# Down projection of a ConvFFN: pass order, place of the last split, and banks of the last token tile

## The chip, the core and the metric

The kernel runs on one core of a Trainium2 chip. The metric is the device time of one execution in microseconds; of several runs the median counts. TensorE (PE) multiplies, VectorE (DVE) and ScalarE (ACT) evict, split and normalise, GpSimd (POOL) does little but issue some transfers, and SyncE (SP) issues most of them.

## The reference

One layer of a decoder trunk on 1024 tokens of width 1024 in float32: a mixer (stick-breaking attention and a short convolution, gated and projected), then a ConvFFN. Only the ConvFFN's end is touched by the change:

```python
h = rms_norm(x, norm_ffn_pre[l])
u = causal_dwconv(h @ w_up[l], conv_ffn_w[l])
a, g = jnp.split(u, 2, axis=-1)
f = (jax.nn.gelu(g, approximate=True) * a) @ w_down[l]
x = x + rms_norm(f, norm_ffn_post[l])
```

w_up is 1024 x 5632, w_down 2816 x 1024. So f has 2816 rows of 1024 tokens before the last product, which are 22 k-tiles of 128.

## The kernel before

**Numbers in two halves.** Each float32 operand is scaled by a power of two and split into two float16 tiles: ScalarE copies the high half (line 100), VectorE subtracts it and keeps the low half (line 101). A product of two such operands has three passes over the halves: (0, 0), (0, 1) and (1, 0), which is `PASSES`; the first number is the half of f, the second that of w_down. The scale comes from a sum of squares per partition that a matmul with ones adds over the partitions (line 83, tile `pr`), and two or three small VectorE instructions (lines 90 to 93).

**The up projection.** For each of the 22 k-tiles of f a pair of up products is computed by seven block products of 12 matmuls each (line 1198, tiles `pu<f>a`, `b` and `c`, one PSUM bank each). Their sums are evicted on ScalarE and VectorE (lines 1213 to 1227), convolved (lines 1272 to 1275), passed through GELU (line 1282), multiplied (line 1283), and their squares summed (line 57, `jk_f`). The f tiles stay in float32 until their group is split.

**The down projection in six bursts.** The 22 k-tiles of f are taken in groups of 2, 4, 4, 4, 4 and 4. One call of `down(g)` multiplies a group's k-tiles by their rows of w_down for all eight token tiles, 128 tokens by 1024 columns each, in two banks of 512 columns: 192 matmuls for a group of four, 96 for the group of two. They are the six bursts of this document, the first to the sixth. Group g's f tiles are split by `f_split(g)` and its rows of w_down are loaded and split by `dn_split(g)`; both are called some products ahead of `down(g)`, during the next group's second pair. In the first four bursts ScalarE copies the sums out (line 1097) and transfers add them up in memory (`yd`); in the fifth VectorE adds the sum loaded from there (line 1099), and in the sixth VectorE adds to that, ScalarE squares (line 1101), VectorE multiplies by the gain (line 1103), sums the squares (line 1109), and after the root (lines 229 and 230) adds the residual (line 1113), half a row at a time, and the result goes out (line 1114).

The last three calls of the FFN are, in this order, `down(ng - 2)`, `f_split(ng - 1)` and `down(ng - 1)`: the fifth burst, the split of the last four f tiles, the sixth burst. Before them stand both remaining `dn_split`.

**Buffers.** The rows of w_down are staged in float32 in a pool of four buffers, `ws`, which the weights of the up products use too (line 1059 for w_down, line 114 for w_up). A staging buffer is free again after VectorE has made the low half out of it. All PSUM banks of the FFN, eight of 512 columns, come from one pool, `pz` (line 1005), for the up products as for the bursts and the `pr` sums. Slots of a slab of sixteen hold f tiles, both kinds of split tiles, the sums of the up products, and at the end the gain, the residual and the output tiles.

**What sets the order.** The FFN is written without an order per engine. A planner lists the instructions: an instruction's priority is its place in the program, and each engine takes, in a simulated time, the first one in priority whose operands and buffers are ready. On the chip each engine then runs its list strictly in order. Matmuls that accumulate into one bank keep the order of the program. `high_priority` (line 1201) lifts the evictions of the up products.

## Time and profile before

| | |
|---|---|
| median of 3 runs | 1318.55 us (1317.56 to 1321.24) |
| profiled execution | 1321.92 us |
| its span | 1320.1 us |
| TensorE busy | 1278.1 us, 97% of the span |
| VectorE busy | 995.3 us, 75% |
| ScalarE busy | 807.3 us, 61% |
| burst matmuls | 1056, idle before them 9.9 us |

The profile shows one execution. A group line has the source line, the engine, the operation, output<-inputs by the names of the tiles without their numbers, the shape and the count, then busy time and mean duration in ns, then the engine's idle time just before them and what ended it. A timeline line has the start and the duration in us, then the same, with the idle time before in square brackets. Matmuls overlap one another in the pipeline: the duration of one is longer than the time from one start to the next. A row with several instructions (x186) spans from the first start to the last end.

### The profile page before, as it was taken

The numbers are of one execution on the slowest core, as the hardware profiler recorded it, in microseconds if no ns is written. First come the engines' busy times: TensorE is split into PE (matmuls) and PEld (weight loads), VectorE is DVE, ScalarE is ACT, GpSimd is POOL, SyncE is SP. The second block draws the span as 40 slices with busy tenths as digits, with TensorE's granted clock in tenths as the row PEclk, the third lists the DMA queues.
The fourth block names the chain that finished last, engine by engine and source line by source line (L and its number), as shares of the span: only waits on it lengthen the run. The fifth ranks groups of instructions, "written<-read, shape, count | busy, mean of one in ns | idle before, by whom it ended". The sixth has DMA issues, their size and how long they took to land. (4 is left out here: it accounts for less than half of the span.)

```text
span 1320.1 us, 16773 instructions
## 1 busy us (share of the span) xinstructions
PE 1278.1 (97%) x6465; PEld 583.7 (44%) x6465; DVE 995.3 (75%) x1584; ACT 807.3 (61%) x1146; POOL 48.6 (4%) x69
## 2 busy tenths in 40 slices
PE   5999999999999999999989999999999999999997
PEld 3444444444444444444544444444444444444443
DVE  5568878797877878796888959917955890798758
ACT  6366575657767666755665677646754764676422
POOL 1000000000000000001100000020010002000001
PEclk9999999999999999999999999999999999999999
DMA  7034535454441212513312252373256239512125
GB/s 272 1 70 104 125 78 115 106 111 94 88 120 49 64 62 68 191 49 112 133 59 65 64 223 64 96 128 128 64 130 157 65 96 209 174 64 96 64 75 196
DMA packets 109391, 139.56 MB, mean 106 GB/s; under 512 B 79088, under 2 KB 79088, under 8 KB 109312
## 3 DMA queue, kind: packets, MB, share of 16 engines
q1 hardware_dynamic: 105360, 124.28, 31.3%
q0 software_dynamic: 3952, 14.23, 6.1%
q8 instruction: 50, 0.82, 0.3%
q14 instruction: 29, 0.24, 0.1%
HBM read 94.45 MB, written 25.17 MB: 91 GB/s over the span
## 5 line engine op out<-in xcount | busy, mean ns | idle before, releaser
L1198 PEld LDWEIGHTS <-wh_u 128*128 128x128 f16 x1848 | 178.7, 98 | 217.7 <-issue 4.0
L1093 PE MATMUL pd<-wdh,f 128*128 128x512 f16 x1056 | 233.9, 383 | 9.9 <-DVE wdh L101 5.7
L1093 PEld LDWEIGHTS <-f 128*128 128x128 f16 x1056 | 104.1, 99 | 138.2 <-issue 13.9
L1198 PEld LDWEIGHTS <-wh_g 128*128 128x128 f16 x588 | 56.9, 98 | 68.7 <-issue 0.4
L908 PE MATMUL py<-wh_wo,m 128*128 128x512 f16 x384 | 83.9, 379 | 0.0
L1097 ACT ACTIVATE y<-pd,sd 128x512 f32<-128x512 f32 x64 | 42.3, 693 | 64.7 <-PE pd L1093 58.3
L101 DVE SCALAR_TENSOR_TENSOR wh_u<-ws_u,sc,wh_u 128x1024 f16<-128x1024 f32 (+1 forms) x66 | 72.3, 1102 | 8.9 <-ACT wh_u L100 8.9
L100 ACT ACTIVATE wh_u<-ws_u,sc 128x1024 f16<-128x1024 f32 (+1 forms) x66 | 64.2, 998 | 22.6 <-DVE ws_u L1033 12.6
L535 ACT ACTIVATE R<-z,cz 128x1024 f32<-128x1024 f32 (+3 forms) x48 | 43.2, 899 | 42.4 <-PE z L531 42.3
L549 DVE TENSOR_TENSOR_SCAN R<-R,edge 128x256 f32<-128x256 f32 (+3 forms) x64 | 49.2, 811 | 19.6 <-ACT R L535 19.5
L90 DVE TENSOR_SCALAR sc<-pr 128x1 int32<-128x1 int32 x47 | 6.8, 153 | 75.0 <-PE pr L83 75.0
L1275 DVE SCALAR_TENSOR_TENSOR ugu<-cgu,cw_g,ugu 128x1023 f32<-128x1023 f32 (+1 forms) x44 | 56.4, 1281 | 8.8 <-ACT ugu L1273 8.6
L1275 DVE SCALAR_TENSOR_TENSOR ua<-cau,cw_a,ua 128x1023 f32<-128x1023 f32 (+1 forms) x44 | 56.3, 1279 | 2.0 <-ACT ua L1273 1.8
L908 PEld LDWEIGHTS <-m 128*128 128x128 f16 x384 | 37.5, 98 | 44.1
L549 DVE TENSOR_TENSOR_SCAN R<-R,cy,zero 128x512 f32<-128x512 f32 x32 | 39.3, 1270 | 12.4 <-ACT R L535 12.4
L57 ACT ACTIVATE jk_u<-ws_u 128x1024 bf16<-128x1024 f32 x44 | 46.5, 1056 | 2.7 <-DMA ws_u<-w_up_nt 2.0
L364 PE MATMUL pv<-wh_v,hT 128*128 128x512 f16 x192 | 45.8, 391 | 2.3 <-ACT wh_v L100 1.7
L262 PE MATMUL pq<-hT,wh_q 128*128 128x512 f16 x192 | 44.2, 379 | 2.1 <-ACT hT L251 1.2
L536 ACT ACTIVATE be<-z,cz 128x1024 f32<-128x1024 f32 (+3 forms) x48 | 43.0, 896 | 4.9 <-DVE R L568 4.8
L1273 ACT ACTIVATE ua<-cau,cw_a 128x1024 f32<-128x1024 f32 x22 | 25.1, 1141 | 34.2 <-DVE cau L1225 31.4
L568 DVE TENSOR_TENSOR R<-be,R 128x1024 f16<-128x1024 f32 (+3 forms) x48 | 45.6, 950 | 0.5 <-ACT R L566 0.2
L558 DVE TENSOR_TENSOR be<-be,R 128x1024 f32<-128x1024 f32 (+3 forms) x48 | 45.7, 953 | 0.1
(666 smaller groups left out, 2521.0 us busy)
## 6 DMA issues: line engine op xcount, KB each, us to landing
ws_u<-w_up_nt SPq DMA_DIRECT2D x44, 512.0 KB, 3.5
yd<-y POOLq DMA_DIRECT2D x24, 512.0 KB, 5.7
ds<-w_down SPq DMA_DIRECT2D x22, 512.0 KB, 6.4
wd<-w_down SPq DMA_DIRECT2D x22, 512.0 KB, 3.5
ws_g<-w_in_nt SPq DMA_DIRECT2D x14, 512.0 KB, 3.5
x<-x SPq DMA_DIRECT2D x8, 512.0 KB, 8.7
ws_wo<-w_out SPq DMA_DIRECT2D x8, 512.0 KB, 6.5
xr<-x SPq DMA_DIRECT2D x8, 512.0 KB, 4.2
```

What stands on the lines that cost most here:

```text
L57: self.nc.scalar.activation(self.junk(f"jk_{name}"), src, AF.Square, accum_out=acc)
L100: self.nc.scalar.activation(dst[:, 0, :], src, AF.Copy, scale=s)
L101: self.nc.vector.scalar_tensor_tensor(dst[:, 1, :], src, s, dst[:, 0, :], ALU.mult, ALU.subtract)
L262: nc.tensor.matmul(ps, w[:, wi, ds(k * P, P)], hT[:, hi, k, ds(c * NH, NH)], start=n == 0, stop=n == last)
L364: nc.tensor.matmul(pv, hT[:, hi, k, ds(tt * P, P)], wv[k // 2][:, wi, ds((k % 2) * NH, NH)], start=n == 0, stop=n == 3 * KD - 1)
L549: nc.vector.tensor_tensor_scan(rev, rev, first, 0.0 if u["top"] else carry[tl][:, h, :], ALU.mult, ALU.add)
L558: nc.vector.tensor_tensor(t["be"][:, :, :W], t["be"][:, :, :W], t["R"][:, :, 1:W + 1], ALU.mult)
L568: nc.vector.tensor_tensor(wv[1], be[:, :, :W], wv[0], ALU.subtract)
L908: nc.tensor.matmul(ps, m16[k][:, hi, ds(tt * P, P)], wo[k][:, wi, sl], start=k == 0 and p == 0, stop=k == 7 and p == 2)
L1093: nc.tensor.matmul(ps, f16[g][k][:, hi, ds(tt * P, P)], w[k][:, wi, sl], start=n == 0, stop=n == 3 * GROUPS[g] - 1)
L1198: nc.tensor.matmul(ps, w[wt][:, wi, ds(wc * NH + k * P, P)], self.block(i, hi, k), start=first and n == 0, stop=n == 3 * KH - 1, skip_grou ...
L1275: nc.vector.scalar_tensor_tensor(u[:, lag:], c[:, :T - lag], sm[:, 2 - lag:3 - lag], u[:, lag:], ALU.mult, ALU.add)
```

## The change

Three edits, all in the down projection:

1. In every burst the order of a bank's matmuls changes from "for each k-tile the passes (0, 0), (0, 1), (1, 0)" to "for each pass of (0, 0), (1, 0), (0, 1) all k-tiles", so that the four products with the low half of w_down are the last. In the first token tile the two banks take turns matmul by matmul; in the other tiles one bank follows the other, as before.
2. `f_split` of the last group is called inside the fifth burst, ahead of the third token tile's matmuls, where before it stood behind the burst.
3. In the sixth burst the last token tile has three banks, of 512, 256 and 256 columns, where it had two of 512; each has its own eviction, square, and gain product, and one more small addition joins the third sum of squares.

```diff
-        def down(g):
+        def down(g, within=None):
...
-                for nh in range(2):
-                    ps = self.bank(f"pd{g}_{tt}_{nh}")
-                    sl = ds(nh * NH, NH)
-                    n = 0
-                    for k in range(GROUPS[g]):
-                        for hi, wi in PASSES:
-                            nc.tensor.matmul(ps, f16[g][k][:, hi, ds(tt * P, P)], w[k][:, wi, sl],
-                                             start=n == 0, stop=n == 3 * GROUPS[g] - 1)
-                            n += 1
+                if tt == 2 and within is not None:
+                    within()
+                cols = [(0, NH), (NH, NH // 2), (NH + NH // 2, NH // 2)] if last and tt == 7 else [(0, NH), (NH, NH)]
+                banks = []
+
+                def products(qs, part):
+
+                    for hi, wi in qs:
+                        for k in range(GROUPS[g]):
+                            for n, (c0, cw) in part:
+                                nc.tensor.matmul(banks[n][:, :cw], f16[g][k][:, hi, ds(tt * P, P)],
+                                                 w[k][:, wi, ds(c0, cw)], start=(hi, wi) == (0, 0) and k == 0,
+                                                 stop=(hi, wi) == (0, 1) and k == GROUPS[g] - 1)
+
+                for n in range(len(cols)):
+                    banks.append(self.bank(f"pd{g}_{tt}_{n}"))
+                order = ((0, 0), (1, 0), (0, 1))
+                if tt == 0:
+                    products(order, list(enumerate(cols)))
+                for n, (c0, cw) in enumerate(cols):
+                    ps, sl = banks[n][:, :cw], ds(c0, cw)
+                    if tt > 0:
+                        products(order, [(n, (c0, cw))])
...
                 if last:
                     nc.vector.tensor_tensor(sm_[:, 0:1], sm_[:, 3:4], sm_[:, 4:5], ALU.add)
+                    if len(cols) > 2:
+                        nc.vector.tensor_tensor(sm_[:, 0:1], sm_[:, 0:1], sm_[:, 5:6], ALU.add)
...
-        down(ng - 2)
-        f_split(ng - 1)
+        down(ng - 2, lambda: f_split(ng - 1))
         down(ng - 1)
```

## The prediction

> **What bounds the kernel now.** I read the page first, then the groups by shape, then TensorE in order of time around the six bursts of the down projection, then its clock there.

> ```profile
> span 1320.1 us, 16773 instructions
> PE 1278.1 (97%) x6465; PEld 583.7 (44%) x6465; DVE 995.3 (75%) x1584; ACT 807.3 (61%) x1146; POOL 48.6 (4%) x69
> L1093 PE MATMUL pd<-wdh,f 128*128 128x512 f16 x1056 | 233.9, 383 | 9.9 <-DVE wdh L101 5.7 <-ACT f L100 2.3 <-DVE cau L1225 1.5
> ```

> TensorE is busy 97% of the span, so a microsecond in which it stands still is a microsecond of the kernel. The bursts' matmuls lose 9.9 us to waits, 5.7 of it for the low half of w_down. The timeline of TensorE shows where (start, duration, count, idle before):

> ```profile
> 745.03 1.24 PE L1093 MATMUL pd<-wdh,f 128*128 128x512 f16 x5
> 747.74 0.38 PE L1093 MATMUL pd<-wdh,f 128*128 128x512 f16 x1 [1.47 <-DVE cau L1225]
> 748.94 5.73 PE L1093 MATMUL pd<-wdh,f 128*128 128x512 f16 x18 [0.82 <-DVE wdh L101]
> 754.50 0.81 PE L1198 MATMUL pu4a<-hA,wh_u 128*128 128x512 f16 x3
> ...
> 842.72 1.46 PE L1093 MATMUL pd<-wdh,f 128*128 128x512 f16 x6
> 844.98 40.30 PE L1093 MATMUL pd<-wdh,f 128*128 128x512 f16 x186 [0.81 <-DVE wdh L101]
> ...
> 957.79 1.46 PE L1093 MATMUL pd<-wdh,f 128*128 128x512 f16 x6
> 961.13 17.00 PE L1093 MATMUL pd<-wdh,f 128*128 128x512 f16 x78 [1.88 <-DVE wdh L101]
> ...
> 1073.94 1.46 PE L1093 MATMUL pd<-wdh,f 128*128 128x512 f16 x6
> 1077.40 41.99 PE L1093 MATMUL pd<-wdh,f 128*128 128x512 f16 x186 [2.00 <-DVE wdh L101]
> ...
> 1226.23 1.89 PE L1093 MATMUL pd<-wdh,f 128*128 128x512 f16 x8 [0.45 <-ACT wdh L100]
> 1228.30 39.87 PE L1093 MATMUL pd<-wdh,f 128*128 128x512 f16 x184 [0.19 <-DVE wdh L101]
> 1268.01 0.17 PE L83 MATMUL pr<-rb,ones 128*128 128x1 bf16 x1
> 1270.45 41.61 PE L1093 MATMUL pd<-wdh,f 128*128 128x512 f16 x192 [2.28 <-ACT f L100]
> ```

> One matmul takes (1268.01 - 1228.30) / 184 = 0.2158 us from start to start. Against that pace the bursts lose, at their heads: first 2.61 (746.11 to 747.74, 747.96 to 748.94), second 0.96 (844.02 to 844.98), third 2.04, fourth 2.16, fifth 0.34 (1227.96 to 1228.30), sixth 2.41. Inside a burst nothing is lost. The clock adds to it; this table of stretches gives after the DVE and ACT columns the granted clock (0.65, 0.54, 1.00), then the DMA share:

> ```profile
> 748.94:752.50 3.56, 3.56 (x11) 1.39 (x11) 3.56 (x5) 2.22 (x3) 0.00 (x0) 0.65 0.64 167
> 1077.40:1080.95 3.55, 3.55 (x10) 1.25 (x10) 3.49 (x4) 1.34 (x2) 0.00 (x0) 0.54 0.57 177
> 1270.45:1312.00 41.55, 41.55 (x192) 18.69 (x192) 34.88 (x62) 13.21 (x32) 4.62 (x7) 1.00 0.50 173
> ```

> After the gaps of the first and fourth burst the clock was down for some 3.55 us, which cost 3.56 x 0.35 = 1.25 and 3.55 x 0.46 = 1.63 us. After the sixth burst's longer gap it was not.

> **Pass order, bursts two to four: a new wait.** A bank's matmuls run in program order. Before, a bank took all three passes of k-tile 0, then of k-tile 1; now it takes f-high x w-high of all four k-tiles before anything else. So the old order needs the low half early, and the new order needs the high halves of k-tiles 2 and 3 early. When do these come? Second burst, all engines:

> ```profile
> 840.73 2.17 ACT L100 ACTIVATE wdh<-wd,sc 128x1024 f16<-128x1024 f32 x2
> 843.64 1.28 DVE L101 SCALAR_TENSOR_TENSOR wdh<-wd,sc,wdh 128x1024 f16<-128x1024 f32 x1
> 844.84 0.69 DVE L1227 TENSOR_TENSOR cgu<-pu7b,cgu 128x512 f32<-128x512 f32 x1
> 844.95 2.12 SPq L1060 DMA_DIRECT2D wd<-w_down  x2
> 848.52 1.15 ACT L100 ACTIVATE wdh<-wd,sc 128x1024 f16<-128x1024 f32 x1 [1.75 <-DMA wd<-w_down]
> 851.14 1.15 ACT L100 ACTIVATE wdh<-wd,sc 128x1024 f16<-128x1024 f32 x1 [1.47 <-DMA wd<-w_down]
> 853.23 0.57 ACT L1213 ACTIVATE cgu<-pu8a 128x512 f32<-128x512 f32 x1
> 857.05 1.27 ACT L1097 ACTIVATE y<-pd,sd 128x512 f32<-128x512 f32 x2 [2.30 <-PE pd L1093]
> ```

> Only two w_down tiles are staged at the start (the four staging buffers also hold the next pair's weights). The load of k-tile 2 leaves at 844.95, just after VectorE's low split of k-tile 0 (843.64 + 1.28 = 844.92) frees its buffer; its high half is there at 848.52 + 1.15 = 849.67, that of k-tile 3 at 852.29. So the low half of k-tile 0, which the edit calls late, comes before the high half of k-tile 2, which it now needs first.

> How much can TensorE do meanwhile? Of the eight banks one holds pu8a through the burst and one pu7b until 844.84 + 0.69 = 845.53: six banks at the start (hence six matmuls before the old wait), then seven. The planner does spread over them: the first finished bank is copied at 857.05, (857.05 - 844.98) / 0.2158 + 6 = 62 matmuls in, where one bank needs 12. Under the old order seven banks hold 7 x 6 = 42 matmuls on k-tiles 0 and 1 (9.1 us); under the new one 7 x 2 = 14 (3.02 us), then nothing until 849.67. Lost: 849.67 - 842.72 - 3.02 = 3.93 us. Seven more matmuls on k-tile 2 (1.51 us) end before k-tile 3's high half: 852.29 - 849.67 - 1.51 = 1.11 more. From there all passes are covered. The same for the third and the fourth burst:

> ```profile
> 962.18 0.69 DVE L1227 TENSOR_TENSOR cgu<-pu11b,cgu 128x512 f32<-128x512 f32 x1
> 964.63 1.15 ACT L100 ACTIVATE wdh<-wd,sc 128x1024 f16<-128x1024 f32 x1 [0.52 <-DMA wd<-w_down]
> 966.77 1.15 ACT L100 ACTIVATE wdh<-wd,sc 128x1024 f16<-128x1024 f32 x1 [0.98 <-DMA wd<-w_down]
> ...
> 1077.26 0.68 DVE L1227 TENSOR_TENSOR cgu<-pu15b,cgu 128x512 f32<-128x512 f32 x1
> 1080.75 1.15 ACT L100 ACTIVATE wdh<-wd,sc 128x1024 f16<-128x1024 f32 x1 [1.63 <-DMA wd<-w_down]
> 1083.02 1.15 ACT L100 ACTIVATE wdh<-wd,sc 128x1024 f16<-128x1024 f32 x1 [1.12 <-DMA wd<-w_down]
> ```

> Third: 965.78 - 957.79 - 3.02 = 4.97 to k-tile 2, then 967.92 - 965.78 - 1.51 = 0.63. Fourth: 1081.90 - 1073.94 - 3.02 = 4.94, then 0.76. At full clock the three lose 13.84 + 2.50 = 16.34 us, where they lost 0.96 + 2.04 + 2.16 + 1.63 = 6.79: 9.55 us worse. With the clock down after each stall the seven k-tile-2 matmuls run at half pace (3.02 us, past k-tile 3's arrival, so the 2.50 vanish) and 1.63 is lost three times: 13.84 + 4.89 = 18.73, 11.94 worse. I take the second: TensorE now does only 3 us of work in the first 7 to 8 us of each burst, emptier than the gaps that brought the clock down before. The first is kept as the bound.

> [...]

> **Bursts one and five.** The first has two k-tiles, the fifth has all four staged:

> ```profile
> 747.45 1.15 ACT L100 ACTIVATE wdh<-wd,sc 128x1024 f16<-128x1024 f32 x1 [1.81 <-DMA wd<-w_down]
> 1225.04 4.25 ACT L100 ACTIVATE wdh<-wd,sc 128x1024 f16<-128x1024 f32 x4
> ```

> In the first the second high half is there at 748.60 instead of the low at 748.94: 0.34 gained, the clock as before. In the fifth the high halves follow each other by 1.06 us while seven banks take 1.51 us of matmuls for each, so the 0.34 us wait goes.

> **The f split inside the fifth burst.** Its sum is ready early:

> ```profile
> 1245.55 0.15 DVE L74 CAST rb<-sc 128x1 bf16<-128x1 f32 x1
> L83 PE MATMUL pr<-rb,ones 128*128 128x1 bf16 x47 | 7.3, 166 | 5.2 <-DVE rb L74 3.8 <-DVE sc_wc L201 1.3
> ```

> The sum's matmul, now ahead of token tile 2 in priority, can go at about 1246 instead of 1268.01; four splits on ACT and DVE then end by about 1255, beside matmuls, and 2.41 us at the sixth burst go. The sum's matmul could itself hold TensorE until the cast: between 0 and 3.6 us (the cast ends at 1245.7; six finished banks, 72 matmuls, could be over at 1242.1). Only two of 47 such matmuls waited in this trace, so I take 0. The f tiles' four slots come free earlier, so the post-norm gain and residual loads behind them only come sooner.

> **Last tile in three banks.** It adds one eviction, square, product and add on 256 or one columns and halves others; 24 matmuls of 256 columns take 12 x 0.2158 us as before, their weight loads hidden as now (18.69 us of loads inside 41.55). The end hangs on VectorE:

> ```profile
> 1312.53 0.74 DVE L1099 SCALAR_TENSOR_TENSOR y<-pd,sd,y 128x512 f32<-128x512 f32 x1
> L373 DVE SCALAR_TENSOR_TENSOR v<-pv,v 128x256 f16<-128x256 f32 x16 | 6.0, 417 | 4.6 <-ACT v L369 4.6
> ```

> The last eviction falls from 0.74 to about 0.42, the square by about 0.2; but another 0.4 eviction and 0.4 product queue ahead of it, and an add of 0.15 behind. Bounds -0.6 to +0.6; I take 0.

> **Sum.** +11.94 - 0.34 - 0.34 - 2.41 = +8.85 us. The profiled execution took 1321.92, 1.82 outside its span and 3.37 over the median; the terms are differences within one execution, so I add them to the median: 1318.55 + 8.85 = 1327.4. At full clock: 1325.0.

> **Rivals.** (a) The planner fills the hole: pu4a's matmuls inside the first burst show that it puts other products there. The decision point is 9.55 - 3.09 = 6.46 us, 2.15 a burst, ten matmuls. With both 12-matmul products (5.18 us) each new hole of at most 5.7 us is all but gone: -6.79 - 3.09 + 0.94 (what is left of 5.60 and 5.70), so 1309.6, faster. With one product: 16.34 - 7.77 - 6.79 - 3.09 = -1.3, 1317.2. Against it: pu8a's next product needs ACT's copy at 853.23, behind both late high halves in ACT's order. (b) The low waits go and no other comes: 1318.55 - 6.79 - 2.61 - 1.25 - 0.34 - 2.41 = 1305.2. For it only that k-tiles 0 and 1 are split before 842.90. (c) The planner's order isn't changed where it matters; bursts one to four wait as before: 1318.55 - 2.75 = 1315.8. (d) It doesn't spread over banks and stands at token tile 0, 4 matmuls in and then two per k-tile: 8.3, 8.8 and 8.9 us at full clock, 26.0 for 16.34: 1334.7 or more; the 62 matmuls speak against it. (e) The sum's matmul holds the fifth burst: 1327.4 + 3.6 = 1331.0.

> **Numbers.** Forecast 0.58; (a) 0.08 with two products, 0.07 with one; (b) 0.06; (c) 0.08; (d) 0.07; (e) 0.06. The forecast's own range is 1323 to 1331; 1311 to 1334 leaves out (b), (d) and a part of (a). About 0.3% (4 us) is what a measurement here tells from no change. Slower by more: 0.58 + 0.07 + 0.06 = 0.71; within: (c) and one product, 0.15; faster: 0.14.

> **What would show it.** In the changed profile, bursts two to four should show TensorE's idle time released by "ACT wdh L100" and no more by "DVE wdh L101", about 14 matmuls before a stall of 2 to 4 us, and a granted clock near 0.5 after it; the sixth burst should follow the fifth without a gap, the sum's matmul standing inside the fifth. I am wrong if the second burst's 192 matmuls take no more than 42.4 us from its first matmul, or if products of the next pair stand in the holes.

## The result, and the profile after

The changed kernel takes 1341.51 us (median of 4 runs, 1339.47 to 1343.38) where the kernel before takes 1318.62: a ratio of 1.0171, 95% interval 1.0155 to 1.0188. It is 22.9 us slower; forecast were 8.9 us slower, with a range from 1311 to 1334. The direction was right and the size was not.

The page of the changed kernel and the group of its burst matmuls of 512 columns (L1097 there is L1093 of before):

```profile
span 1341.6 us, 16801 instructions
PE 1286.1 (96%) x6477; PEld 586.6 (44%) x6477; DVE 996.5 (74%) x1587; ACT 807.5 (60%) x1148; POOL 47.9 (4%) x69
L1097 PE MATMUL pd<-wdh,f 128*128 128x512 f16 x1044 | 238.1, 390 | 15.6 <-ACT wdh L100 9.2 <-DVE cgu L1242 4.9 <-DVE cau L1240 1.5
```

The low half of w_down (DVE wdh) is gone from the waits, as the change wants it. In its place stand 9.2 us for the high half (ACT wdh) and 4.9 us for a bank. The bursts in order of time:

```profile
749.20 5.34 PE L1097 MATMUL pd<-wdh,f 128*128 128x512 f16 x24 [0.56 <-ACT wdh L100]
...
841.30 3.45 PE L1097 MATMUL pd<-wdh,f 128*128 128x512 f16 x14
848.29 41.45 PE L1097 MATMUL pd<-wdh,f 128*128 128x512 f16 x178 [3.54 <-ACT wdh L100]
...
962.25 2.75 PE L1097 MATMUL pd<-wdh,f 128*128 128x512 f16 x12
967.28 0.59 PE L1097 MATMUL pd<-wdh,f 128*128 128x512 f16 x2 [2.27 <-DVE cgu L1242]
970.23 40.23 PE L1097 MATMUL pd<-wdh,f 128*128 128x512 f16 x178 [2.36 <-ACT wdh L100]
...
1082.97 2.75 PE L1097 MATMUL pd<-wdh,f 128*128 128x512 f16 x12
1088.31 0.59 PE L1097 MATMUL pd<-wdh,f 128*128 128x512 f16 x2 [2.59 <-DVE cgu L1242]
1091.15 41.20 PE L1097 MATMUL pd<-wdh,f 128*128 128x512 f16 x178 [2.25 <-ACT wdh L100]
...
1239.19 11.05 PE L1097 MATMUL pd<-wdh,f 128*128 128x512 f16 x48 [0.45 <-ACT wdh L100]
1258.55 0.16 PE L83 MATMUL pr<-rb,ones 128*128 128x1 bf16 x1 [8.31 <-DVE rb L74]
1258.57 75.25 PE L1097 MATMUL pd<-wdh,f 128*128 128x512 f16 x348
```

Two things are to be seen. Bursts two to four do 14 matmuls and then stand still until k-tile 2's high half is there (the third and the fourth also wait after 12 of the 14, for a bank). And the fifth does 48, two token tiles, and then waits 8.31 us for the sum of the last f group; after it the sixth follows without a gap. With the first burst starting at 745.56 in this execution, the two traces differ like this, from the start of one burst to the start of the next:

| stretch | before, us | after, us | difference | forecast |
|---|---|---|---|---|
| to the first burst | 745.03 | 745.56 | +0.53 | 0 |
| first to second | 97.69 | 95.74 | -1.95 | -0.34 |
| second to third | 115.07 | 120.95 | +5.88 | +4.60 |
| third to fourth | 116.15 | 120.72 | +4.57 | +4.56 |
| fourth to fifth | 152.29 | 156.22 | +3.93 | +2.78 |
| fifth to the end | 93.87 | 102.41 | +8.54 | -2.75 |
| span | 1320.1 | 1341.6 | +21.5 | +8.85 |

The clock fell behind the new stalls (stretches of time, the granted clock is the third number from the right):

```profile
848.29:854.50 6.21, 6.21 (x16) 2.27 (x16) 5.38 (x6) 3.61 (x4) 0.00 (x0) 0.53 0.45 147
970.23:977.00 6.77, 6.77 (x24) 2.73 (x24) 6.73 (x8) 3.62 (x4) 0.00 (x0) 0.75 0.39 137
1091.15:1098.00 6.85, 6.85 (x20) 2.62 (x20) 6.81 (x8) 3.61 (x4) 0.00 (x0) 0.61 0.45 136
1258.57:1264.50 5.93, 5.93 (x17) 2.21 (x17) 4.72 (x8) 4.27 (x4) 0.56 (x1) 0.56 0.14 45
```

Why does the sum come so late? ScalarE and VectorE of the changed kernel in the fifth burst:

```profile
1244.66 1.15 ACT L100 ACTIVATE wdh<-wd,sc 128x1024 f16<-128x1024 f32 x1 [1.37 <-DMA wd<-w_down]
1247.82 1.15 ACT L100 ACTIVATE wdh<-wd,sc 128x1024 f16<-128x1024 f32 x1 [2.01 <-DMA wd<-w_down]
1249.51 2.38 ACT L100 ACTIVATE wdh<-wd,sc 128x1024 f16<-128x1024 f32 x2 [0.54 <-DMA wd<-w_down]
1251.79 1.04 ACT L1297 ACTIVATE ugu<-ugu 128x1024 f32<-128x1024 f32 x1
1256.97 1.06 ACT L57 ACTIVATE jk_f<-ua 128x1024 bf16<-128x1024 f32 x1 [4.14 <-DVE ua L1298]
...
1248.30 1.28 DVE L1290 SCALAR_TENSOR_TENSOR ugu<-cgu,cw_g,ugu 128x1022 f32<-128x1022 f32 x1
1251.89 2.72 DVE L1113 SCALAR_TENSOR_TENSOR y<-pd,sd,y 128x512 f32<-128x512 f32 x4
1254.52 1.28 DVE L101 SCALAR_TENSOR_TENSOR wdh<-wd,sc,wdh 128x1024 f16<-128x1024 f32 x1
1255.71 1.22 DVE L1298 TENSOR_TENSOR ua<-ugu,ua 128x1024 f32<-128x1024 f32 x1
1258.34 0.16 DVE L74 CAST rb<-sc 128x1 bf16<-128x1 f32 x1
```

The cast starts 1258.34 - 1239.19 = 19.15 us into the burst, as before (1245.55 - 1226.23 = 19.32). The last f tile's GELU (L1297) stands on ScalarE behind the four high halves of the sixth group, and these wait for their loads: its operand is there at 1248.30 + 1.28 = 1249.58, and it starts 2.21 us later. The product behind it (L1298) waits again, for VectorE: GELU ends at 1252.83, and the product starts 2.88 us later, behind four evictions of the fifth burst and a low half of the sixth group's w_down.

### The profile page after: what moved, and what is told of

It reads as the page before. It is cut to its first block, busy times and chain, and to the rows that moved or that the text cites. A ratio compares the mean times of both kernels' runs of the same rounds, so it can differ in the third digit from the quotient of the medians.

```text
span 1341.6 us, 16801 instructions
## 1 busy us (share of the span) xinstructions
PE 1286.1 (96%) x6477; PEld 586.6 (44%) x6477; DVE 996.5 (74%) x1587; ACT 807.5 (60%) x1148; POOL 47.9 (4%) x69
## 5 line engine op out<-in xcount | busy, mean ns | idle before, releaser
L1213 PEld LDWEIGHTS <-wh_u 128*128 128x128 f16 x1848 | 178.7, 98 | 217.7 <-issue 4.0
L1097 PE MATMUL pd<-wdh,f 128*128 128x512 f16 (+1 forms) x1068 | 240.7, 388 | 15.6 <-ACT wdh L100 9.2
L1097 PEld LDWEIGHTS <-f 128*128 128x128 f16 x1068 | 106.8, 100 | 156.9 <-issue 40.4
L1213 PEld LDWEIGHTS <-wh_g 128*128 128x128 f16 x588 | 56.9, 98 | 68.7 <-issue 0.4
L100 ACT ACTIVATE wh_u<-ws_u,sc 128x1024 f16<-128x1024 f32 (+1 forms) x66 | 64.1, 997 | 24.3 <-DVE ws_u L1033 14.8
L101 DVE SCALAR_TENSOR_TENSOR wh_u<-ws_u,sc,wh_u 128x1024 f16<-128x1024 f32 (+1 forms) x66 | 72.1, 1101 | 8.1 <-ACT wh_u L100 8.1
L90 DVE TENSOR_SCALAR sc<-pr 128x1 int32<-128x1 int32 x47 | 6.8, 152 | 85.4 <-PE pr L83 85.3
L1115 ACT ACTIVATE jf<-y 128x512 bf16<-128x512 f32 (+1 forms) x17 | 10.3, 606 | 60.5 <-DVE y L1113 59.9
```

The lines of the kernel that those rows point to most:

```text
L100: self.nc.scalar.activation(dst[:, 0, :], src, AF.Copy, scale=s)
L101: self.nc.vector.scalar_tensor_tensor(dst[:, 1, :], src, s, dst[:, 0, :], ALU.mult, ALU.subtract)
L1097: nc.tensor.matmul(banks[n][:, :cw], f16[g][k][:, hi, ds(tt * P, P)], w[k][:, wi, ds(c0, cw)], start=(hi, wi) == (0, 0) and k == 0, stop=( ...
L1213: nc.tensor.matmul(ps, w[wt][:, wi, ds(wc * NH + k * P, P)], self.block(i, hi, k), start=first and n == 0, stop=n == 3 * KH - 1, skip_grou ...
```

## The experiments

The theory after the result: (1) in bursts two to four the high halves of k-tiles 2 and 3 starve TensorE, since their loads wait for staging buffers; (2) the sum's matmul holds the fifth burst, since the token tiles behind it in the program can't pass it. Each comparison is with runs of the kernel before on the same chip.

### The three edits, each by itself

Only the place of the split, in the old pass order:

```diff
+                if tt == 2 and within is not None:
+                    within()
...
-        down(ng - 2)
-        f_split(ng - 1)
+        down(ng - 2, lambda: f_split(ng - 1))
```

> Only the split of the last f group is moved into the fifth burst (ahead of token tile 2); the pass order and the two banks stay as before. Theory: the matmul of the sum stands right behind token tiles 0 and 1, 48 matmuls in, and TensorE waits there for the cast, which comes some 19.5 us after the burst's start: (1226.23 + 19.5) - (1226.23 + 0.34 + 48 x 0.2158) = 8.8 us lost, about 2.6 more at the lowered clock, 2.4 gained at the sixth burst: 1318.6 + 9.0 = 1327.6 us. Rival (all of the loss is the pass order, and the moved split gains as predicted): 1316.2 us.

Measured: 1327.15 us against 1320.43, ratio 1.0043 (1.0026 to 1.0060). The profile has the wait behind 4 + 44 = 48 matmuls:

```profile
1225.16 1.02 PE L1095 MATMUL pd<-wdh,f 128*128 128x512 f16 x4 [0.45 <-ACT wdh L100]
1227.23 9.66 PE L1095 MATMUL pd<-wdh,f 128*128 128x512 f16 x44 [1.05 <-DVE wdh L101]
1244.76 0.16 PE L83 MATMUL pr<-rb,ones 128*128 128x1 bf16 x1 [7.87 <-DVE rb L74]
```

So this edit alone makes the kernel slower, by some 6 us where 9.0 were expected. In the profiled execution the stretch from the fifth burst's start to the end took 1328.0 - 1225.16 = 102.84 us, 8.97 more than the 93.87 before, as the theory has it; why the medians show less isn't settled.

Only the pass order:

```diff
-        down(ng - 2, lambda: f_split(ng - 1))
+        down(ng - 2)
+        f_split(ng - 1)
...
-                cols = [(0, NH), (NH, NH // 2), (NH + NH // 2, NH // 2)] if last and tt == 7 else [(0, NH), (NH, NH)]
+                cols = [(0, NH), (NH, NH)]
```

> Only the pass order (with the two banks of the first token tile in turns); the split of the last f group stands behind the fifth burst and the last token tile has two banks. Theory: bursts two to four lose 14.4 us as in the changed kernel, the first gains 0.3 to 1.9, the fifth 0.3: 1318.6 + 12.6 = 1331.2 us (1329 to 1334), and the sixth burst's gap of 2.3 us is back. Rival (the split is what costs, and the order only as much as at full clock was forecast, 9.5): 1327 us or less.

Measured: 1335.82 us against 1320.43, ratio 1.0112 (1.0096 to 1.0127). The order is the larger part. It is some 2 to 3 us over the expected 12.6. The gap ahead of the sixth burst is back, and in the profiled execution the clock fell after it, which it didn't in the kernel before (the second row is a stretch of time, as above):

```profile
1281.94 43.30 PE L1097 MATMUL pd<-wdh,f 128*128 128x512 f16 x192 [2.28 <-ACT f L100]
1281.94:1285.50 3.56, 3.56 (x11) 1.41 (x12) 3.56 (x3) 3.06 (x3) 0.00 (x0) 0.65 1.01 376
```

That is 43.30 - 41.61 = 1.69 us for the same 192 matmuls.

Only the three banks of the last token tile:

```diff
-                    for hi, wi in qs:
-                        for k in range(GROUPS[g]):
+                    for k in range(GROUPS[g]):
+                        for hi, wi in qs:
...
-                order = ((0, 0), (1, 0), (0, 1))
+                order = PASSES
-                if tt == 0:
+                if False:
...
-                    if tt > 0:
+                    if True:
...
-        down(ng - 2, lambda: f_split(ng - 1))
+        down(ng - 2)
+        f_split(ng - 1)
```

> Only the last token tile in three banks; pass order and place of the split as before. Theory (prediction's term): no change, -0.6 to +0.6 us against the kernel before; the last eviction 0.42 to 0.48 in place of 0.74 us, but one eviction and one product more queue ahead of it on VectorE. Rival (the shorter tail counts): 0.5 us or more faster.

Measured: 1320.44 us against 1319.31, ratio 1.0007 (0.9998 to 1.0015): no difference that can be told.

### The fifth burst

The split ahead of token tile 5 in place of 2, and ahead of token tile 3:

```diff
-                if tt == 2 and within is not None:
+                if tt == 5 and within is not None:
```

> The changed kernel with the split called ahead of token tile 5 in place of 2, 120 matmuls (25.9 us) into the fifth burst, after the cast (about 19.3 us in). Theory: TensorE no longer waits for the sum, 9.0 + 2.6 us come back and the gap ahead of the sixth burst stays closed: 1341.5 - 11.6 = 1329.9 us. Rival (the wait in the fifth burst is lost time that turns up elsewhere, as VectorE is late there anyway): 1336 us or more.

> The changed kernel with the split ahead of token tile 3 in place of 2. Theory: the sum's matmul stands 72 matmuls in (15.5 us), the cast comes 19.3 us in: TensorE waits 3.8 us in place of 9.0, and the clock costs 1.6 to 2.6 us as before: 1341.5 - 5.2 - 0.5 = 1335.8 us (1335 to 1337). Rival (the wait follows the late cast wherever the matmul stands): the wait stays at 8 us.

Measured: ahead of tile 5, 1331.29 us against 1320.43, ratio 1.0078 (1.0063 to 1.0093); ahead of tile 3, 1335.81 against 1319.31, ratio 1.0128 (1.0113 to 1.0142). Against the changed kernel's 1.0171 the first gives back 0.93%, 12.3 us. The fifth burst, tile 5 first, then tile 3:

```profile
1238.84 26.06 PE L1097 MATMUL pd<-wdh,f 128*128 128x512 f16 x120 [0.45 <-ACT wdh L100]
1264.74 0.17 PE L83 MATMUL pr<-rb,ones 128*128 128x1 bf16 x1
1264.77 57.17 PE L1097 MATMUL pd<-wdh,f 128*128 128x512 f16 x276
```

```profile
1238.21 15.70 PE L1097 MATMUL pd<-wdh,f 128*128 128x512 f16 x72 [0.45 <-ACT wdh L100]
1258.01 0.16 PE L83 MATMUL pr<-rb,ones 128*128 128x1 bf16 x1 [4.09 <-DVE rb L74]
```

The sum's matmul stands exactly where the program has it, 120 and 72 matmuls in, and the wait is what is left until the cast: 8.31 us at 48, 4.09 at 72, none at 120. The cast stays where it was (19.15, 19.59 and 19.90 us into the burst), so the matmul's place decides.

Why do tiles 2 to 7 not pass it? A bank of its own for the sums, the other tiles sharing seven:

```diff
-        self.pz = pm = self.top.enter_context(tc.tile_pool(name="pz", bufs=8, space=bass.MemoryType.PSUM))
-        self.sum_psum = (pm, [P, NH], "pm")
+        self.pz = pm = self.top.enter_context(tc.tile_pool(name="pz", bufs=7, space=bass.MemoryType.PSUM))
+        self.sum_psum = (self.top.enter_context(tc.tile_pool(name="prp", bufs=1, space=bass.MemoryType.PSUM)), [P, NH], "pr")
```

> The changed kernel with the split at token tile 2, but the sums' matmuls have a PSUM bank of their own and all other tiles share seven. Theory: the sum's matmul held the fifth burst because token tiles 2 to 7 get their banks from the same pool after it; with its own bank it stands 111 matmuls (24 us) into the burst, after the cast at about 19.3 us: the 9.0 + 2.6 us come back, less about 0.4 us in each of bursts two to four, which have two matmuls less to do while they wait: 1341.5 - 11.6 + 1.3 = 1331.2 us. Rival (its place follows from the program order alone): 1341 us or more, with the wait of 8 us.

Measured: 1340.02 us against 1319.31, ratio 1.0160 (1.0145 to 1.0176). By its time alone this would speak for the rival; the profile shows two effects that nearly cancel:

```profile
748.01 0.16 PE L83 MATMUL pr<-rb,ones 128*128 128x1 bf16 x1 [0.73 <-DVE sc L90]
750.96 1.69 PE L1097 MATMUL pd<-wdh,f 128*128 128x512 f16 x6 [2.79 <-ACT wdh L100]
...
1247.10 24.12 PE L1097 MATMUL pd<-wdh,f 128*128 128x512 f16 x111 [0.45 <-ACT wdh L100]
1271.05 0.17 PE L83 MATMUL pr<-rb,ones 128*128 128x1 bf16 x1
```

In the fifth burst the sum's matmul now stands 111 matmuls in, behind tiles 2 and 3 and part of 4, with no wait: with a bank of its own it no longer holds them. From the burst's start to the end it is 1338.4 - 1247.10 = 91.30 us, 11.11 less than in the changed kernel. But the fifth burst starts 7.91 us later than there (1247.10 against 1239.19), where 1.3 us were expected for bursts two to four. These cost 0.76 us more; the rest is lost earlier, 5.40 us up to the first burst's start (750.96 against 745.56) and 1.75 from there to the second. Just ahead of the first burst a sum's matmul waits 0.73 us until VectorE has read the sum before it (L90), as all sums now share one bank, and the burst then waits 2.79 us for its high half. No run has seven banks with the sums still among them, so the smaller pool and the sums' own bank aren't told apart.

What makes the cast late? The split of the sixth group's w_down moved behind that of f, inside the fifth burst:

```diff
-        dn_split(ng - 1, True)
-        down(ng - 2, lambda: f_split(ng - 1))
+        down(ng - 2, lambda: (f_split(ng - 1), dn_split(ng - 1, True)))
```

> The changed kernel with the split of the sixth group's w_down rows moved too: it stands behind the split of the f tiles, ahead of token tile 2, and no longer ahead of the fifth burst. Theory: the cast comes 19.3 us into the burst because the last f tile's GELU stands on ScalarE behind four high halves that wait for their loads; without these the chain of conversion, GELU, product, squares and cast ends 13 to 16 us in, TensorE waits 3 to 5.5 us in place of 8.9 ahead of token tile 2: 1341.5 - 3.4 to 5.9 = 1336 to 1338 us. Rival (the cast is late through VectorE's own queue): the wait stays at 8 us, 1341 us.

Measured: 1336.72 us against 1319.53, ratio 1.0132 (1.0116 to 1.0148). GELU and the sum's matmul there (the row of two is this sum and the one of w_down's squares):

```profile
1236.74 11.05 PE L1097 MATMUL pd<-wdh,f 128*128 128x512 f16 x48 [0.47 <-ACT wdh L100]
1246.15 1.06 ACT L1296 ACTIVATE ugu<-ugu 128x1024 f32<-128x1024 f32 x1 [5.30 <-DVE ugu L1289]
1251.35 0.22 PE L83 MATMUL pr<-rb,ones 128*128 128x1 bf16 x2 [3.56 <-DVE rb L74]
```

GELU starts 9.41 us into the burst where it started 12.60 us in, and the sum's matmul comes 14.61 us in where it came 19.36 us in; the wait shrinks to 3.56 us. Both explanations have a part in these 4.75 us, since the edit takes low halves out of VectorE's way as well as high halves out of ScalarE's. GELU starts 0.10 us after its operand in place of 2.21, which is the part of the late loads (2.1 us). Its operand comes 1.1 us earlier and the product follows it after 0.64 us in place of 2.88 (2.2 us), which is VectorE's own queue; behind the product 0.7 us are lost again. So the time came out as expected, but the theory's cause is the smaller part.

### Bursts two to four

K-tiles 2 and 3 of groups 1 to 3 staged in tiles of another pool, so that their loads need no staging buffer back:

```diff
-                t = self.ws.tile([P, D], F32, tag="ws", name=f"wd2_{g}_{i}")
+                t = self.ws.tile([P, D], F32, tag="ws", name=f"wd2_{g}_{i}") if i < 2 or g in (0, 4, 5) else \
+                    self.xp.tile([P, D], F32, tag="x", name=f"wd2_{g}_{i}")
```

> The changed kernel, but in groups 1 to 3 the w_down rows of k-tiles 2 and 3 are staged in two tiles of the pool that later holds the sums of the last token tiles, and not in the four staging buffers; so their loads and high halves no longer wait for the low halves of k-tiles 0 and 1. Theory: TensorE's waits for ACT wdh in bursts two to four vanish (21.3 us lost there now, nothing then), the 8 to 9 us wait in the fifth stays: 1341.5 - 21.3 = 1320.2 us. Rival (the pass order starves TensorE whatever the staging): 1338 us or more.

Measured: 1321.43 us against 1319.31, ratio 1.0018 (1.0009 to 1.0027): of the 1.71% that the changed kernel loses 1.53 are gone, 20.2 us (21.3 were expected). Its bursts:

```profile
839.53 41.60 PE L1098 MATMUL pd<-wdh,f 128*128 128x512 f16 x192
953.64 41.60 PE L1098 MATMUL pd<-wdh,f 128*128 128x512 f16 x192
1067.75 41.60 PE L1098 MATMUL pd<-wdh,f 128*128 128x512 f16 x192
1216.19 11.05 PE L1098 MATMUL pd<-wdh,f 128*128 128x512 f16 x48 [0.45 <-ACT wdh L100]
1235.55 0.16 PE L83 MATMUL pr<-rb,ones 128*128 128x1 bf16 x1 [8.31 <-DVE rb L74]
```

With the same pass order, bursts two to four now run their 192 matmuls in one piece; the fifth waits as in the changed kernel. Low half last is sound where all four high halves are there in time. The two causes add up: this edit gives back 1.53%, the split ahead of tile 5 gives back 0.93%, and both together (the last run below) 2.29%, the same within the intervals.

The new order in the first token tile alone, the old one in the other seven (with the split ahead of tile 5):

```diff
-                    for hi, wi in qs:
-                        for k in range(GROUPS[g]):
+                    ks = range(GROUPS[g])
+                    steps = [(k, q) for q in qs for k in ks] if tt == 0 else [(k, q) for k in ks for q in PASSES]
+                    for i, (k, (hi, wi)) in enumerate(steps):
```

> The new pass order in the first token tile alone (two banks in turns, low half last), the old order in the other seven; the split ahead of token tile 5, three banks for the last tile. Theory: while the high half of k-tile 2 is on its way the other five banks work through all passes of k-tiles 0 and 1, so the long waits for ACT wdh go; what is left is the wait for the first low half, after 8 matmuls in place of 6: 0.5, 1.6 and 1.7 us in bursts two to four, with or without a lowered clock: 1319.3 - 2.8 - 0.3 - 0.3 - 2.4 = 1313.5 us (1311.5 to 1315.5). Rival (the turns in the first tile are enough to starve TensorE): 1325 us or more.

Measured: 1312.77 us against 1319.53, ratio 0.9953 (0.9938 to 0.9967): faster than the kernel before. The third and the fourth burst wait less than the 1.6 and 1.7 us expected: one wait of 0.42 us is left in the third, none that the trace lists in the fourth. Two short waits are left in the second (0.5 us were expected):

```profile
845.30 7.28 PE L1098 MATMUL pd<-wdh,f 128*128 128x512 f16 x33 [0.37 <-DVE wdh L101]
852.74 9.44 PE L1098 MATMUL pd<-wdh,f 128*128 128x512 f16 x43 [0.16 <-ACT wdh L100]
```

So the turns in the first tile starve nothing; the order of the seven tiles behind it does: the run with the split ahead of tile 5 differs from this one in that order alone, and its ratio is 1.0078.

### Two versions that beat both kernels

Low half last within each pair of k-tiles, the split ahead of tile 5:

```diff
-                    for hi, wi in qs:
-                        for k in range(GROUPS[g]):
+                    for k0 in range(0, GROUPS[g], 2):
+                        for hi, wi in qs:
+                            for k in (k0, k0 + 1):
...
-                if tt == 2 and within is not None:
+                if tt == 5 and within is not None:
```

> The changed kernel, but the three passes run over k-tiles 0 and 1 first and over 2 and 3 after them, low half last within each pair; the split is called ahead of token tile 5. Theory: seven banks have 7 x 4 = 28 matmuls (6.0 us) before a low half is needed and 42 (9.1 us) before the high half of k-tile 2, so bursts two to four wait for nothing: 1318.6 - 6.8 (their waits and lowered clock) - 0.3 to 1.9 (first burst) - 0.3 (fifth) - 2.4 (sixth) = 1308 us (1306 to 1310). Rival (low half last starves TensorE in any grouping, through the turns of the two banks): 1320 us or more.

Measured: 1310.53 us against 1320.43, ratio 0.9922 (0.9907 to 0.9937). The heads of bursts two to four and, last, the sixth without a gap (the remaining 72 matmuls of the fifth, then the sixth):

```profile
841.77 18.29 PE L1098 MATMUL pd<-wdh,f 128*128 128x512 f16 x84
...
955.88 18.29 PE L1098 MATMUL pd<-wdh,f 128*128 128x512 f16 x84
...
1069.99 18.29 PE L1098 MATMUL pd<-wdh,f 128*128 128x512 f16 x84
...
1244.36 57.17 PE L1098 MATMUL pd<-wdh,f 128*128 128x512 f16 x276
```

84 matmuls in 18.29 us are the full pace (84 x 0.2158, and 0.16 more for the last, which takes 0.38). The staging of k-tiles 2 and 3 in tiles of their own with the split ahead of tile 5, that is the staging experiment's edit and `tt == 5`:

```diff
...
+                    self.xp.tile([P, D], F32, tag="x", name=f"wd2_{g}_{i}")
...
-                if tt == 2 and within is not None:
+                if tt == 5 and within is not None:
```

> The changed kernel's pass order in all tiles with k-tiles 2 and 3 of groups 1 to 3 staged in tiles of their own (as in e6) and the split ahead of token tile 5. Theory: both waits are gone: 1319.3 + 2.1 (e6) - 11.6 = 1309.8 us (1308 to 1312), the same as the grouping in pairs. Rival (early staging costs something that the wait for the sum covered): 1315 us or more.

Measured: 1310.67 us against 1319.53, ratio 0.9942 (0.9925 to 0.9958). Which of the two is the better can't be told from these intervals.

## Why the prediction was wrong in size and right in sign

**Pass order, bursts two to four: right.** The step that the new order needs the high halves of k-tiles 2 and 3 early, and that these wait for the low halves of 0 and 1, is shown by the staging experiment. Its numbers held too: 14 matmuls before k-tile 2, and the time to k-tile 2 cost 848.29 - 841.30 - 3.02 = 3.97, 970.23 - 962.25 - 3.02 = 4.96 and 1091.15 - 1082.97 - 3.02 = 5.16 us where 3.93, 4.97 and 4.94 were forecast. The clock's term was too small: 178 matmuls at full pace take 38.41 us, so the rows of 41.45, 40.23 and 41.20 us (0.16 less each from start to start) lost 2.88, 1.66 and 2.63, together 7.2 for the 4.89 of the forecast, any short rest of a wait included. All in all +14.4 for +11.94.

**The f split: the step that failed.** The prediction said that "the sum's matmul, now ahead of token tile 2 in priority, can go at about 1246", took 0 for its wait and bounded it at 3.6 us. It saw the condition (the matmul can hold TensorE until the cast), named it as rival (e) with 0.06, and got its place wrong: it took six finished banks, 72 matmuls, as the work ahead of it (six banks are what VectorE had evicted before the cast in the profile of before), as if the matmul's place followed from these. Its place follows from the program, 48 matmuls in, 72 one tile later. What keeps the tiles behind it from passing is the pool of banks that they share with it, as the own-bank run shows (which takes a bank from the other tiles as well); by what rule the planner does so isn't shown. 1239.19 + 48 x 0.2158 = 1249.55 against a cast at 1258.34 is 8.8 us, and these numbers stood in the profile of before: a cast 19.3 us into the burst against 48 x 0.2158 = 10.4 us of work. The frequency from which 0 was taken, two of 47 sums that wait, said nothing on this one, which was moved ahead of its operand. The wait and the lowered clock behind it cost 9.0 + 2.6 us, for the 2.41 us that it did save at the sixth burst.

**The rest.** The first burst gained 1.95 us for 0.34; in this execution its gap was not followed by a lower clock (1.00 from 749.20 to 753.00), which the kernel before paid with some 1.25 us. That part is luck and not the change: with the split alone and with the three banks alone, both in the old order, the 18 matmuls behind the same gap took 4.04 us, where before they took 5.73. The 1.63 us that the forecast took off for the clock in the fourth burst are read from the one profiled execution of the kernel before, too. The fifth burst's low-half wait went, as said. The three banks made no difference, as said. Rivals (a), (b), (c) and (d) fall: no product of the next pair stands in the holes of bursts two to four, new waits came, the order changed where it mattered, and the bursts spread over seven banks.

## What to carry to other kernels

Before an operand is put last, look at what its consumer then needs first, and whether that comes out of the buffers which the late operand gives back. Before an instruction is moved ahead in an engine that runs in order, compare the work that is ahead of it in its new place with the time its operand needs from the same start: moved to 120 matmuls the split won (ratio 1.0078, against 1.0112 with the new order alone), at 48 it cost 11.6 us and saved 2.4. Both numbers could be read in the profile of before.

## What the runs showed of the hardware

After the changed kernel's 8.31 us wait the 0.56 is the mean of a stretch of 5.93 us. In shorter stretches the clock was 0.50 until 1263.50 and 1.00 from 1264.00, so it was down for some 5 us after the wait; in the fourth burst of before, after a gap of 2.00 us, it was 0.50 from 1078.00 to 1081.00 and back at 1.00 from 1081.10, 3.7 us after the gap.
